# HGRN2 intra-chunk scores: 64 query columns per score matmul, shared PSUM banks, and a head's TensorE work in six bursts

## The chip, the cores and the metric

The kernel runs on one core of a Trainium2 chip. Its metric is the device time of one execution in microseconds (us). A core has five engines that run their own instruction queues in order: TensorE (PE, with its weight loads shown as PEld), VectorE (DVE), ScalarE (ACT), GpSimd (POOL) and SyncE (SP). Matmul results land in PSUM; the kernel keeps eight tiles of [128, 512] float32 there, one bank each, four for the projections (pool `pj`) and four for everything else (pool `pm`).

## What is computed

Two residual layers on a [512, 2048] float32 input: a recurrent layer (Griffin RG-LRU beside HGRN2, one input and one output projection), then differential attention. The part that matters is HGRN2, with 16 heads of 128 features, in chunks of 64 tokens:

```python
b = jnp.cumsum(gc, axis=2)                                   # log decay inside a chunk
o_inter = jnp.einsum('bhtk,bhkv->bhtv', qc * jnp.exp(b), state)
decay = jnp.exp(jnp.where(mask, b[:, :, :, None, :] - b[:, :, None, :, :], -jnp.inf))
scores = jnp.einsum('bhtk,bhsk,bhtsk->bhts', qc, kc, decay)
o = o_inter + jnp.einsum('bhts,bhsv->bhtv', scores, vc)
state = (jnp.exp(b_last[:, :, 0, :, None]) * state
         + jnp.einsum('bhsk,bhsv->bhkv', kc * jnp.exp(b_last - b), vc))
```

## The kernel before

Every projection is done in float32 by three float32r products of split operands: `split` (L91, L92) makes the weight tiles `whi` on ACT and `wlo` on DVE, five buffers each, and `mm3` (L104 to L106) multiplies. A raw weight chunk gives two half chunks of 12 matmuls with 512 columns each; these are the `pj` matmuls of the trace. All input projections of the HGRN2 heads come first (pairs of heads, 24 half chunks for q, f and gate, and 16 more for v in every second pair), then those of RG-LRU, then the output projection, then attention.

A head's own work is a Python generator, `hgrn_head`. After each half chunk, `tick(2)` runs two steps of the oldest unfinished head (a step ends at a `yield`). Before, a head has 24 steps, so two heads fill 24 half chunks. The Tile scheduler then orders each engine's queue, with the weight splits at high priority; it may move a step's instructions past some projection matmuls.

Inside a chunk the decay is not separable, so scores are built by levels of half block size h = 32, 16, 8, 4, 2, each from one tile `e` [128 features, 512 tokens]: in every block of 2h tokens the first h columns hold decayed keys and the last h decayed queries. `decays(h)` makes it: two subtractions or additions on DVE (L238, L239), an Exp on ACT (L240), a product with q on DVE (L241). `scores` multiplies `e` with itself, for h < 32 in four 128 x 128 products (L258); a float32 matmul is two instructions on PE, so one level is 8 LDWEIGHTS and 8 MATMUL. `copy_predicated` (L265) then takes the query columns of the level's blocks into the score tile `st`. The level h = 32 uses eight 32 x 32 products (L251). The products for s = t and s = t - 1 are sums over the features by a matrix of ones (L271 to L277).

After the levels come the 64 x 64 products between the two chunks of a 128-token pair (L318), transposes of the decayed keys `kp` (L325), the state products (L332, each followed by a DVE update, L334 and L336), the output product of scores and state (L343, L345) and its norm. The norm is: four squares with a sum on ACT (L350), a reciprocal square root by Newton steps on DVE (L115 to L122, twelve small instructions in a chain), the product `kp <- pm, rs_y` on DVE (L354), four transposes on PE (L359), and the product with gain and gate (L363). On ACT the functions Exp, Ln and Silu lie in different tables; a change of table is an ACT_TABLE_LOAD instruction in ACT's queue. The log decay of the next head takes Abs, Exp, Ln on ACT (L206 to L208) and then L209 on DVE.

Of the kernel before, what the change touches and what calls it, by code (L numbers as in the profile page):

```python
# [19 lines left out]
P = 128  # L20
# [15 lines left out]
# steps of the heads' own work between two half chunks of a projection  # L36
# [10 lines left out]
# columns of the packed constants  # L47
# [4 lines left out]
class Kernel:  # L52
# [73 lines left out]
    def proj_feat(self, h, src, chunk0, ticks):  # L126
        """256 output features as two [feature, token] banks"""
# [13 lines left out]
    def proj_tok(self, lhs, order, src, chunk0, ticks):  # L141
        """512 output features as four [token, feature] banks; lhs(kt) gives the split activations"""
# [14 lines left out]
    def prepare(self):  # L157
        """1 / rms of each token, as columns and as a row repeated for every partition; small constants"""
# [37 lines left out]
    def hgrn_head(self, hd, qs, f, sg, v, vc):  # L196
        nc, wk, sm, pm = self.nc, self.wk, self.sm, self.pm
        V = nc.vector
        # the lower bound is a softmax over one layer less its first row: it is zero
        # for these shapes, so log_f = log_sigmoid(f) and k = sigmoid(-f)  # L200
# [10 lines left out]
        # the scale of q goes with k  # L211
# [5 lines left out]
        # s = t, and s = t - 1 for odd t: products summed over the features by ones  # L217
# [26 lines left out]
        def scores(li, h, e):  # L244
            ps = pm.tile([P, S], F32, name="pm")
            if h == 32:
                ev, pv = (y.rearrange("p (a c) -> p a c", a=NT) for y in (st, ps))
# [5 lines left out]
                for o in (0, 64):  # L253
                    V.tensor_copy(ev[o:o + 32, :, o + 32:o + 64], pv[o:o + 32, :, o + 32:o + 64])
# [6 lines left out]
            def v4(t):  # L261
                return t.rearrange("p (a n two h) -> p a n two h", a=NT, two=2, h=h)[:, :, :, 1, :]
# [18 lines left out]
        yield
        for li, h in enumerate(LEVELS[1:], 1):
            pend.append((li, h, decays(h)))
            yield
            scores(*pend.pop(0))
            yield
        # pairs of 64-token chunks: k decayed to the end of its even chunk, q from the start of
        # its odd one; then both for the 128-token chunks, which meet through a running state
# [33 lines left out]
        so = wk.tile([P, 768], F32, name="so")
        ps = pm.tile([P, S], F32, name="pm")
        for c in range(NT - 1):
            nc.tensor.transpose(ps[:, c * P:(c + 1) * P], kp[:, c * P:(c + 1) * P], self.ident)  # L325
        nc.scalar.copy(so[:, 0:384], ps[:, 0:384])
# [75 lines left out]
    def rg_lambda(self):  # L402
        """-8 * softplus(-lambda), with log1p as 2 atanh(e / (2 + e))"""
# [24 lines left out]
    def rg_head(self, hd, xr, sg):  # L428
# [110 lines left out]
    def att_pair(self, pr, q, k, v, box):  # L539
# [7 lines left out]
        def heads_in(hh):  # L547
            """split transposes of a head's q and k"""
# [148 lines left out]
    def run(self):  # L697
# [20 lines left out]
        with ExitStack() as st:  # L718
# [3 lines left out]
            # products that nothing reads warm the array up while the first loads are under way  # L722
# [43 lines left out]
            # x1 = x + y @ w_out, its split transpose times the gain, and its mean squares  # L766
# [83 lines left out]
def feat_chunks(w, c0):  # L850
    """[2048, 256] at column c0 -> 4 chunks of four k tiles"""
# [3 lines left out]
def tok_chunks(w, c0, order=None):  # L855
    """[k, 512] at column c0 -> chunks of two k tiles, in the order of use"""
# [7 lines left out]
def layout(x, rec_norm, rec_w_in, rg_conv_w, rg_conv_b, rg_w_gate_a, rg_b_gate_a, rg_w_gate_x, rg_b_gate_x,  # L864
# [14 lines left out]
    gate = np.stack([rg_w_gate_a[0], rg_w_gate_x[0]], 1)                     # head, gate, i, j  # L879
# [41 lines left out]
```

## Time and profile before

| what | value |
|---|---|
| time, median of 3 runs (lowest to highest) | 2596.68 us (2595.3 to 2596.8) |
| span of the profiled execution | 2594.6 us |
| PE busy | 2579.6 us (99%), 12416 MATMUL |
| PEld busy | 2126.2 us (82%), 12416 LDWEIGHTS |
| DVE busy, ACT busy | 1417.0 us (55%), 1258.6 us (49%) |
| granted TensorE clock, mean | 0.998 of 2.4 GHz |
| L258 MATMUL, the score levels | 512, 67.5 us busy |
| L240 Exp of the levels on ACT | 80, 50.5 us busy |

The span of the profiled execution is 2.1 us under the median. A MATMUL's duration includes a part that overlaps with the next one, so what an instruction costs is read from the distance between starts, not from its duration. Starts are given to 0.01 us in the timelines.

### The profile page before, as it was taken

What the parts mean: (1) busy time and instruction counts of PE and PEld (TensorE: products, weight loads), DVE (VectorE), ACT (ScalarE), POOL (GpSimd) and SP (SyncE); (2) the same over time, 40 slices, a digit from 0 to 9 for tenths busy, and PEclk for the clock granted to TensorE, in tenths of its full rate; (3) what the DMA queues carried; (4) which work ended last, traced back from release to release, by engine and by line L of the source; (5) the groups of instructions that cost most, each with busy time, mean ns of one, the idle gap of its engine ahead of it and who ended that gap; (6) DMA issues with size and microseconds to landing.
All of it is one profiled execution on the core that took longest, in us unless ns stands there. A gap on an engine that the chain in (4) does not pass through costs nothing.

```text
span 2594.6 us, 33221 instructions
## 1 busy us (share of the span) xinstructions
PE 2579.6 (99%) x12416; PEld 2126.2 (82%) x12416; DVE 1417.0 (55%) x3073; ACT 1258.6 (49%) x2458; POOL 4.6 (0%) x12
## 2 busy tenths in 40 slices
PE   9999999999999999999999999999999999999999
PEld 7888888888888888888888888888888888888887
DVE  5466557646646665545654555344544534544654
ACT  8445545535444455556544444334434434534543
POOL 0000000000000000000000000000000000000000
PEclk9999999999999999999999999999999999999999
DMA  6222222222222222222232333222222222222243
GB/s 244 96 74 82 81 82 74 81 90 74 76 95 74 74 98 102 97 93 98 90 128 95 127 130 120 98 98 75 81 97 77 79 91 82 76 95 93 86 146 114
DMA packets 73457, 250.48 MB, mean 97 GB/s; under 512 B 8144, under 2 KB 8656, under 8 KB 73296
## 3 DMA queue, kind: packets, MB, share of 16 engines
q1 hardware_dynamic: 71712, 243.58, 26.8%
q0 software_dynamic: 1152, 4.19, 0.4%
q8 instruction: 97, 1.59, 0.2%
q10 hardware_dynamic: 432, 0.59, 0.1%
q14 instruction: 64, 0.52, 0.1%
HBM read 239.95 MB, written 8.39 MB: 96 GB/s over the span
## 4 chain that ended last, share of the span: by engine, by line
PE 94%; DVE 2%; ACT 2%; DMA 1%; issue 1%; SPq 0%; ACTq 0%
PE pj L104 28%; PE pj L106 28%; PE pj L105 28%; PE pm L258 2%; PE pm L570 1%; PE pm L104 1%; PE pm L106 1%; PE pm L105 1%; PE pm L343 1%; PE pm L554 1%; DMA yb<-in_x 0%; PE pm L332 0%; PE pm L345 0%; ACT a L675 0%; PE pm L359 0%
## 5 line engine op out<-in xcount | busy, mean ns | idle before, releaser
L92 DVE TENSOR_TENSOR wlo<-wraw,whi 128x512 fp32r<-128x512 f32 x848 | 582.3, 688 | 671.4 <-ACT whi L91 641.2
L91 ACT CAST whi<-wraw 128x512 fp32r<-128x512 f32 x848 | 523.0, 618 | 765.0 <-PE pj L106 463.7
L106 PE MATMUL pj<-whi,wlo 128*128 128x512 f32 x768 | 299.6, 390 | 0.0
L105 PE MATMUL pj<-wlo,whi 128*128 128x512 f32 x768 | 299.4, 390 | 0.0
L104 PE MATMUL pj<-whi 128*128 128x512 f32 x768 | 299.3, 390 | 0.0
L106 PEld LDWEIGHTS pj<-whi,wlo 128*128 128x128 f32 x768 | 144.2, 188 | 30.5 <-DVE wlo L92 0.6
L104 PEld LDWEIGHTS pj<-whi 128*128 128x128 f32 x768 | 144.2, 188 | 30.4 <-issue 0.5
L105 PEld LDWEIGHTS pj<-wlo,whi 128*128 128x128 f32 x768 | 144.2, 188 | 29.1
L240 ACT ACTIVATE e<-e 128x512 f32<-128x512 f32 x80 | 50.5, 632 | 131.7 <-DVE e L239 97.6
L92 DVE TENSOR_TENSOR wlo<-ya,whi 128x512 fp32r<-128x512 f32 x64 | 44.3, 693 | 89.9 <-ACT whi L91 89.9
L92 DVE TENSOR_TENSOR wlo<-y,whi 128x512 fp32r<-128x512 f32 x64 | 44.2, 691 | 82.3 <-ACT whi L91 82.3
L91 ACT CAST whi<-ya 128x512 fp32r<-128x512 f32 x64 | 39.7, 621 | 100.9 <-PE pj L105 100.9
L91 ACT CAST whi<-y 128x512 fp32r<-128x512 f32 x64 | 39.9, 623 | 94.1 <-PE pj L105 90.2
L92 DVE TENSOR_TENSOR wlo<-yb,whi 128x512 fp32r<-128x512 f32 x64 | 44.1, 690 | 72.2 <-ACT whi L91 72.0
L91 ACT CAST whi<-yb 128x512 fp32r<-128x512 f32 x64 | 39.8, 621 | 76.5 <-PE pj L105 76.5
L258 PEld LDWEIGHTS pm<-e 128*128 128x128 f32 x512 | 66.6, 191 | 5.0 <-DVE e L241 0.3
L258 PE MATMUL pm<-e 128*128 128x128 f32 x512 | 67.5, 275 | 0.0
L241 DVE TENSOR_TENSOR e<-e,hin 128x256 f32<-128x256 f32 x80 | 33.6, 420 | 58.8 <-ACT e L240 58.8
L575 ACT ACTIVATE p<-pm,mx 128x128 f32<-128x128 f32 (+3 forms) x64 | 33.7, 526 | 40.6 <-DVE mx L573 38.6
L572 DVE TENSOR_REDUCE mx<-pm 128x1 f32<-128x128 f32 (+3 forms) x64 | 30.4, 485 | 32.6 <-PE pm L571 32.3
L675 ACT ACTIVATE a<-pj,rstd 128x128 f32<-128x128 f32 x128 | 47.3, 421 | 0.3
L104 PE MATMUL pj<-h0h,whi 128*128 128x512 f32 x80 | 33.8, 423 | 5.2 <-DVE hin L384 2.9
(474 smaller groups left out, 6483.0 us busy)
## 6 DMA issues: line engine op xcount, KB each, us to landing
wraw<-in_w_rec SPq DMA_DIRECT2D x192, 512.0 KB, 3.2
wraw<-in_w_att SPq DMA_DIRECT2D x128, 512.0 KB, 3.2
wraw<-in_w_rout SPq DMA_DIRECT2D x64, 512.0 KB, 3.2
wraw<-in_w_aout SPq DMA_DIRECT2D x32, 512.0 KB, 3.2
yb<-in_xT SPq DMA_DIRECT2D x8, 512.0 KB, 8.5
yb<-in_x POOLq DMA_DIRECT2D x8, 512.0 KB, 5.5
wraw<-in_w_gate SPq DMA_DIRECT2D x8, 512.0 KB, 3.2
xo<-in_x SPq DMA_DIRECT2D x16, 256.0 KB, 4.0
```

Of the source, the lines that this page charges most:

```text
L91: self.nc.scalar.copy(hi, src)
L92: self.nc.vector.tensor_tensor(lo, src, hi.bitcast(F32), op=ALU.subtract)
L104: mm(out, a[0], b[0], start=start, stop=False)
L105: mm(out, a[0], b[1], start=False, stop=False)
L106: mm(out, a[1], b[0], start=False, stop=stop)
L240: nc.scalar.activation(e, e, AF.Exp)
L241: V.tensor_tensor(e1, e1, vw(qs, h)[:, :, 1, :], op=ALU.mult)
L258: nc.tensor.matmul(ps[:, sl], e[:, sl], e[:, sl], start=True, stop=True)
L343: nc.tensor.matmul(po[:, sl], st[:, sl], v[:, t, vc:vc + P], start=True, stop=t == 0)
L572: V.tensor_reduce(mx[:, i:i + 1], ps[:, :n], axis=AX.X, op=ALU.max)
L575: nc.scalar.activation(e[:, :n], ps[:, :n], AF.Exp, scale=ATT_SCALE, bias=mx[:, i:i + 1], accum_out=z[:, i:i + 1])
L675: nc.scalar.activation(x[:, t, g * P:(g + 1) * P], ps[t][:, g * P:(g + 1) * P], AF.Square, scale=r1, accum_out=ss[:, t * 4 + g:t * 4 + g + 1])
```

## The change

The tile `e` and its making stay as they are. `scores` becomes two functions. `score_mm` multiplies all 128 columns of a block of `e` as weights with only its 64 query columns (a strided view) as the moving operand, and writes 64 columns. Two levels of 256 columns share one bank. The level h = 32 writes 32 columns for each token tile beside the s = t - 1 sums in the same bank. `score_out` copies from the packed columns. The steps are regrouped: the sums and h = 32 in one step, h = 16 and 8 in one, and h = 4, h = 2, the 64 x 64 products and the transposes of `kp` in one, with three banks. A head has 22 steps instead of 24. Comments are removed; nothing else is touched.

```diff
-        def scores(li, h, e):
-            ps = pm.tile([P, S], F32, name="pm")
+        def score_mm(h, e, ps):
             if h == 32:
...
-                        nc.tensor.matmul(ps[o:o + 32, c + 32:c + 64], e[:, c:c + 32], e[:, c + 32:c + 64],
+                        nc.tensor.matmul(ps[o:o + 32, t * 32:(t + 1) * 32], e[:, c:c + 32], e[:, c + 32:c + 64],
                                          start=True, stop=True)
...
-                nc.tensor.matmul(ps[:, sl], e[:, sl], e[:, sl], start=True, stop=True)
+                nc.tensor.matmul(ps[:, t * 64:(t + 1) * 64], e[:, sl], vw(e[:, sl], h)[:, :, 1, :],
+                                 start=True, stop=True)
+
+        def score_out(li, h, ps):
...
+            dst = st.rearrange("p (a n two h) -> p a n two h", a=NT, two=2, h=h)[:, :, :, 1, :]
             mk = self.msk[:, li * 64:(li + 1) * 64].rearrange("p (n h) -> p n h", h=h)
-            V.copy_predicated(v4(st), mk.unsqueeze(1).broadcast_to([P, NT, n4, h]), v4(ps))
+            V.copy_predicated(dst, mk.unsqueeze(1).broadcast_to([P, NT, n4, h]),
+                              ps.rearrange("p (a n h) -> p a n h", a=NT, h=h))
...
+        e32 = decays(32)
+        yield
+        e16 = decays(16)
         yield
...
+        score_mm(32, e32, p2[:, 256:384])
...
+        score_out(0, 32, p2[:, 256:384])
+        yield
+        e8 = decays(8)
+        yield
+        e4 = decays(4)
+        yield
...
+        score_mm(16, e16, ps[:, 0:256])
+        score_mm(8, e8, ps[:, 256:512])
+        score_out(1, 16, ps[:, 0:256])
+        score_out(2, 8, ps[:, 256:512])
+        yield
+        e2 = decays(2)
+        yield
...
+        score_mm(4, e4, ps[:, 0:256])
+        score_mm(2, e2, ps[:, 256:512])
         for t in range(NT):
-            nc.tensor.matmul(ps[0:64, t * P + 64:(t + 1) * P], ke[:, t, :], qo[:, t, :], start=True, stop=True)
+            nc.tensor.matmul(p2[0:64, t * 64:(t + 1) * 64], ke[:, t, :], qo[:, t, :], start=True, stop=True)
+        for c in range(NT - 1):
+            nc.tensor.transpose(p3[:, c * P:(c + 1) * P], kp[:, c * P:(c + 1) * P], self.ident)
...
+        nc.scalar.copy(so[:, 0:384], p3[:, 0:384])
+        yield
         yield
```

In the changed file the lines shift: L258 becomes L255 (`score_mm`), L318 is L337, L325 is L339, L332 is L352, L343 and L345 are L363 and L365, L350 is L370, L354 is L374, L359 is L379 and L384 is L404. L91, L92, L104 to L106, L115 to L122 and L206 to L209 keep their numbers.

How it moves the rows, for the sixth head (the second of its pair). First PE's queue before, around the last score level and the 64 x 64 products (L258 scores, L318 and L325 as above, the rest projection):

```order
L106 MATMUL pj<-h7h,wlo 128x512
L258 MATMUL pm<-e 128x128 x4
L104 MATMUL pj<-h8h,whi 128x512
L105 MATMUL pj<-h8l,whi 128x512
L106 MATMUL pj<-h8h,wlo 128x512
```

and, twelve projection matmuls further on:

```order
L105 MATMUL pj<-h9l,whi 128x512
L106 MATMUL pj<-h9h,wlo 128x512
L318 MATMUL pm<-e_3370 64x64 x4
L325 MATMUL pm<-cst,kp 128x128 x3
L104 MATMUL pj<-h10h,whi 128x512
L105 MATMUL pj<-h10l,whi 128x512
```

PE's queue now, at the same place of the same head:

```order
L105 MATMUL pj<-h5l,whi 128x512
L106 MATMUL pj<-h5h,wlo 128x512
L255 MATMUL pm<-e 128x64 x8
L337 MATMUL pm<-e_3273 64x64 x4
L339 MATMUL pm<-cst,kp 128x128 x3
L104 MATMUL pj<-h6h,whi 128x512
```

Two levels, the 64 x 64 products and the transposes now stand in one piece, where three pieces stood with twelve projection matmuls between each two.

DVE's queue before, from the first sums of the norm's chain to its end (L354), in the same head:

```order
L122 SCALAR_TENSOR_TENSOR rs_y<-rs_t,rs_y 128x4
L384 TENSOR_TENSOR hin_3530<-pj,rrow 128x512
L120 TENSOR_TENSOR rs_t<-rs_y 128x4
L227 TENSOR_TENSOR e_3592<-so,e_3586 128x768
L92 TENSOR_TENSOR wlo<-wraw,whi 128x512
L121 TENSOR_TENSOR rs_t<-rs_t,rs_m 128x4
L313 TENSOR_TENSOR qp<-qp,hin_3027 128x4x64
L122 SCALAR_TENSOR_TENSOR rs_y<-rs_t,rs_y 128x4
L120 TENSOR_TENSOR rs_t<-rs_y 128x4
L121 TENSOR_TENSOR rs_t<-rs_t,rs_m 128x4
L122 SCALAR_TENSOR_TENSOR rs_y<-rs_t,rs_y 128x4
L92 TENSOR_TENSOR wlo<-wraw,whi 128x512
```

DVE's queue now, at the same place, up to L374:

```order
L122 SCALAR_TENSOR_TENSOR rs_y<-rs_t,rs_y 128x4
L227 TENSOR_TENSOR e_3574<-so,e_3568 128x768
L92 TENSOR_TENSOR wlo<-wraw,whi 128x512
L120 TENSOR_TENSOR rs_t<-rs_y 128x4
L121 TENSOR_TENSOR rs_t<-rs_t,rs_m 128x4
L209 SCALAR_TENSOR_TENSOR lf<-hin_3293,lf 128x512
L122 SCALAR_TENSOR_TENSOR rs_y<-rs_t,rs_y 128x4
L374 TENSOR_TENSOR kp<-pm,rs_y 128x512
```

Now L209 of the next head stands inside the chain, between its last L121 and L122; before, it came after L354. On ACT the instructions that L209 waits for stand like this now, behind the squares of the same norm:

```order
L222 ACTIVATE so<-lf 128x256
L311 ACTIVATE qp<-b 128x512
L206 ACTIVATE lf<-hin_3293 128x512
L225 CAST e_3568<-so 128x768
L91 CAST whi<-wraw 128x512
L207 ACTIVATE lf<-lf 128x512
L208 ACT_TABLE_LOAD
L208 ACTIVATE lf<-lf 128x512
```

Before, L207 and L208 of the next head came three splits later, after L354's place. PE's transposes L379 stand 29 projection matmuls behind the head's output product in the second head of a pair (L359 stood 34 behind) and 23 in the first (27 before). In the whole program ACT has 132 ACT_TABLE_LOAD rows, where it had 118; from RG-LRU's later heads on, the queues are the same as before.

## Rows read from the trace of the kernel before

**Rows 1.** Windows view, the steady part of the HGRN2 stage: length, then busy us of PE, PEld, DVE, ACT, POOL with the number of instructions, granted clock, DMA share, GB/s.

```profile
175.00:915.00 740.00, 738.52 (x3957) 611.89 (x3956) 461.79 (x1068) 365.08 (x680) 0.00 (x0) 1.00 0.23 79
```

**Rows 2.** The chain of work that ended last, shares of the span by engine (from the page).

```profile
PE 94%; DVE 2%; ACT 2%; DMA 1%; issue 1%; SPq 0%; ACTq 0%
```

**Rows 3.** Groups by line, shapes kept apart, from 130 to 915 us: the score levels and the 64 x 64 products. Columns: line, engine, operation, names, weights' size, shape, count, busy us, mean ns of one, idle before.

```profile
L258 PE MATMUL pm<-e 128*128 128x128 f32 x512 | 67.5, 275 | 0.0
L258 PEld LDWEIGHTS pm<-e 128*128 128x128 f32 x512 | 66.6, 191 | 5.0 <-DVE e L241 0.3
...
L318 PE MATMUL pm<-e 128*64 128x64 f32 x128 | 10.9, 228 | 0.0
L318 PEld LDWEIGHTS pm<-e 128*64 128x64 f32 x128 | 8.6, 137 | 5.4 <-PE pj L105 5.3
```

**Rows 4.** Timeline of PE in the HGRN2 stage: start us, length us, engine, line, operation, names, shape, count. A row with x8 or x16 runs from the first start to the last end.

```profile
401.02 1.05 PE L258 MATMUL pm<-e 128*128 128x128 f32 x8
401.83 0.48 PE L104 MATMUL pj<-h6h,whi 128*128 128x512 f32 x1
402.14 0.39 PE L105 MATMUL pj<-h6l,whi 128*128 128x512 f32 x1
...
404.44 0.39 PE L106 MATMUL pj<-h7h,wlo 128*128 128x512 f32 x1
...
408.40 0.68 PE L318 MATMUL pm<-e 128*64 128x64 f32 x8
...
419.93 0.39 PE L104 MATMUL pj<-h0h,whi 128*128 128x512 f32 x1
...
422.42 0.39 PE L106 MATMUL pj<-h1h,wlo 128*128 128x512 f32 x1
...
429.45 0.40 PE L104 MATMUL pj<-h6h,whi 128*128 128x512 f32 x1
...
432.01 0.39 PE L106 MATMUL pj<-h7h,wlo 128*128 128x512 f32 x1
432.32 0.45 PE L251 MATMUL pm<-e 128*32 128x32 f32 x16
432.70 0.50 PE L104 MATMUL pj<-h8h,whi 128*128 128x512 f32 x1
433.04 0.39 PE L105 MATMUL pj<-h8l,whi 128*128 128x512 f32 x1
```

**Rows 5.** Timeline of PE in the attention stage, where L571 adds the causal mask with a bfloat16 matmul of 128 columns and a projection matmul with 128 float32r weight columns follows.

```profile
1759.27 0.23 PE L571 MATMUL pm<-neg_b,ident_b 128*128 128x128 bf16 x1
...
1759.62 0.39 PE L105 MATMUL pj<-wlo,h5h 128*128 128x512 f32 x1
```

**Rows 6.** Timeline of PE and DVE in the first head of a pair, from the output product (L343) to the transposes (L359), and of PE at the transposes of the last head of all. In brackets: idle before, and what ended it.

```profile
162.44 0.61 PE L343 MATMUL pm<-v,st 128*128 128x128 f32 x4
...
165.73 0.42 DVE L223 TENSOR_TENSOR so<-so,hin 128x256 f32<-128x256 f32 x1
...
169.26 0.16 DVE L121 TENSOR_TENSOR rs_t<-rs_t,rs_m 128x4 f32<-128x4 f32 x1
...
169.45 0.16 DVE L122 SCALAR_TENSOR_TENSOR rs_y<-rs_t,rs_y 128x4 f32<-128x4 f32 x1
...
169.65 0.69 DVE L354 TENSOR_TENSOR kp<-pm,rs_y 128x512 f32<-128x512 f32 x1
...
169.95 0.39 PE L106 MATMUL pj<-h10h,wlo 128*128 128x512 f32 x1
...
170.26 0.68 DVE L92 TENSOR_TENSOR wlo<-wraw,whi 128x512 fp32r<-128x512 f32 x1
...
170.49 0.63 PE L359 MATMUL pm<-cst,kp 128*128 128x128 f32 x4 [0.15 <-DVE kp L354]
...
913.82 0.39 PE L106 MATMUL pj<-h6h,wlo 128*128 128x512 f32 x1
914.49 0.63 PE L359 MATMUL pm<-cst,kp 128*128 128x128 f32 x4 [0.28 <-DVE kp L354]
```

**Rows 7.** Timeline of PE, ACT and DVE in the second head of a pair, from the output product on.

```profile
415.61 0.61 PE L343 MATMUL pm<-v,st 128*128 128x128 f32 x4
...
418.38 0.45 ACT L222 ACTIVATE so<-lf 128x256 f32<-128x256 f32 x1
...
420.55 0.62 ACT L91 CAST whi<-wraw 128x512 fp32r<-128x512 f32 x1
...
424.69 0.39 PE L104 MATMUL pj<-h3h,whi 128*128 128x512 f32 x1
...
425.09 0.63 PE L359 MATMUL pm<-cst,kp 128*128 128x128 f32 x4
425.47 0.63 ACT L207 ACTIVATE lf<-lf 128x512 f32<-128x512 f32 x1
...
426.00 0.61 ACT L91 CAST whi<-wraw 128x512 fp32r<-128x512 f32 x1
426.63 1.28 ACT L208 ACT_TABLE_LOAD   x1
427.92 0.63 ACT L208 ACTIVATE lf<-lf 128x512 f32<-128x512 f32 x1
...
428.58 0.69 DVE L209 SCALAR_TENSOR_TENSOR lf<-hin,lf 128x512 f32<-128x512 f32 x1 [0.88 <-ACT lf L208]
```

More of the change, by code (lines that the diff above doesn't have):

```diff
@@ L242, in decays @@
             return e
-        def scores(li, h, e):
-            ps = pm.tile([P, S], F32, name="pm")
+        def score_mm(h, e, ps):
             if h == 32:
-                ev, pv = (y.rearrange("p (a c) -> p a c", a=NT) for y in (st, ps))
                 for t in range(NT):
@@ L257, in scores @@
                 sl = slice(t * P, (t + 1) * P)
-                nc.tensor.matmul(ps[:, sl], e[:, sl], e[:, sl], start=True, stop=True)
+                nc.tensor.matmul(ps[:, t * 64:(t + 1) * 64], e[:, sl], vw(e[:, sl], h)[:, :, 1, :],
+                                 start=True, stop=True)
+        def score_out(li, h, ps):
+            if h == 32:
+                ev, pv = st.rearrange("p (a c) -> p a c", a=NT), ps.rearrange("p (a c) -> p a c", a=NT)
+                for o in (0, 64):
+                    V.tensor_copy(ev[o:o + 32, :, o + 32:o + 64], pv[o:o + 32])
+                return
             n4 = P // (2 * h)
-            def v4(t):
-                return t.rearrange("p (a n two h) -> p a n two h", a=NT, two=2, h=h)[:, :, :, 1, :]
+            dst = st.rearrange("p (a n two h) -> p a n two h", a=NT, two=2, h=h)[:, :, :, 1, :]
             mk = self.msk[:, li * 64:(li + 1) * 64].rearrange("p (n h) -> p n h", h=h)
-            V.copy_predicated(v4(st), mk.unsqueeze(1).broadcast_to([P, NT, n4, h]), v4(ps))
-        pend = [(0, LEVELS[0], decays(LEVELS[0]))]
+            V.copy_predicated(dst, mk.unsqueeze(1).broadcast_to([P, NT, n4, h]),
[3 more added lines that the diff above has]
+        e16 = decays(16)
         yield
@@ L270, in hgrn_head @@
         ps = pm.tile([P, S], F32, name="pm")
+        p2 = pm.tile([P, S], F32, name="pm")
         nc.tensor.matmul(ps, self.ones, xh[:, 0:512], start=True, stop=False)
         nc.tensor.matmul(ps, self.ones, xl[:, 0:512], start=False, stop=True)
+        nc.tensor.matmul(p2[:, 0:256], self.ones, xh[:, 512:768], start=True, stop=False)
+        nc.tensor.matmul(p2[:, 0:256], self.ones, xl[:, 512:768], start=False, stop=True)
+        score_mm(32, e32, p2[:, 256:384])
         V.tensor_tensor(st.rearrange("p (a c) -> p a c", a=NT), ps.rearrange("p (a c) -> p a c", a=NT),
                         self.ident.unsqueeze(1).broadcast_to([P, NT, P]), op=ALU.mult)
-        ps = pm.tile([P, S], F32, name="pm")
-        nc.tensor.matmul(ps[:, 0:256], self.ones, xh[:, 512:768], start=True, stop=False)
-        nc.tensor.matmul(ps[:, 0:256], self.ones, xl[:, 512:768], start=False, stop=True)
         V.copy_predicated(st.rearrange("p (a n two) -> p a n two", a=NT, two=2)[:, :, :, 1],
                           self.msk[:, 64 * len(LEVELS):].unsqueeze(1).broadcast_to([P, NT, 64]),
-                          ps[:, 0:256].rearrange("p (a n) -> p a n", a=NT))
+                          p2[:, 0:256].rearrange("p (a n) -> p a n", a=NT))
+        score_out(0, 32, p2[:, 256:384])
         yield
[L282 to L286, printed above, removed]
+        e8 = decays(8)
+        yield
+        e4 = decays(4)
+        yield
         kp = wk.tile([P, S], F32, name="kp")
@@ L305, in hgrn_head @@
         nc.scalar.activation(qp, b, AF.Exp)
+        yield
+        ps = pm.tile([P, S], F32, name="pm")
+        score_mm(16, e16, ps[:, 0:256])
[5 more added lines that the diff above has]
+        yield
         nc.scalar.activation(ke, c64(kp)[:, :, 0, :], AF.Exp)
         nc.scalar.activation(c64(kp)[:, :, 1, :], c64(kp)[:, :, 1, :], AF.Exp)
+        V.tensor_tensor(qo, c64(qp)[:, :, 1, :], c64(qs)[:, :, 1, :], op=ALU.mult)
         yield
-        scores(*pend.pop(0))
-        yield
-        V.tensor_tensor(qo, c64(qp)[:, :, 1, :], c64(qs)[:, :, 1, :], op=ALU.mult)
         V.tensor_tensor(c64(kp)[:, :, 0, :], ke, dc[:, 1:8:2].unsqueeze(2).broadcast_to([P, 4, 64]), op=ALU.mult)
@@ L315, in hgrn_head @@
         yield
+        yield
         ps = pm.tile([P, S], F32, name="pm")
+        p2 = pm.tile([P, S], F32, name="pm")
+        p3 = pm.tile([P, S], F32, name="pm")
+        score_mm(4, e4, ps[:, 0:256])
+        score_mm(2, e2, ps[:, 256:512])
         for t in range(NT):
-            nc.tensor.matmul(ps[0:64, t * P + 64:(t + 1) * P], ke[:, t, :], qo[:, t, :], start=True, stop=True)
+            nc.tensor.matmul(p2[0:64, t * 64:(t + 1) * 64], ke[:, t, :], qo[:, t, :], start=True, stop=True)
+        for c in range(NT - 1):
+            nc.tensor.transpose(p3[:, c * P:(c + 1) * P], kp[:, c * P:(c + 1) * P], self.ident)
+        score_out(3, 4, ps[:, 0:256])
+        score_out(4, 2, ps[:, 256:512])
         nc.scalar.copy(st.rearrange("p (a c) -> p a c", a=NT)[0:64, :, 64:128],
-                       ps.rearrange("p (a c) -> p a c", a=NT)[0:64, :, 64:128])
+                       p2[0:64, 0:256].rearrange("p (a c) -> p a c", a=NT))
+        so = wk.tile([P, 768], F32, name="so")
+        nc.scalar.copy(so[:, 0:384], p3[:, 0:384])
         yield
[L322 to L326, printed above, removed]
         yield
```

2 lines of the change are left out of this document (removed).

## The prediction

> **What bounds the kernel now.** I read first the windows of the HGRN2 stage, since the change touches nothing else. In 740 us of it PE is busy for 738.52 us at a granted clock of 1.00, DVE for 462 and ACT for 365 [rows 1], and the chain that ended last is 94% PE [rows 2]. So time is won here by a shorter PE queue, and lost where PE has to wait. Next I read the groups of the score levels [rows 3], then PE's timeline around the pieces that the change merges [rows 4], one place in the attention stage that shows what a short moving operand is worth [rows 5], and last the two places where PE waits in every head: the transposes L359 [rows 6, 7].
>
> **The score matmuls stream half the columns: no gain.** A level costs 8 pairs of LDWEIGHTS and MATMUL. Eight MATMULs take 401.83 - 401.02 = 0.81 us to the next projection matmul; inside, starts are (1.05 - 0.275) / 7 = 0.111 us apart [rows 3, 4]. The L318 products, with half the weight columns and half the moving columns, are (0.68 - 0.228) / 7 = 0.065 us apart, an upper end since the first is longer [rows 3, 4]. The question is which of the two halves buys this. The change halves only the moving columns; the weights are still all 128 columns of a block. A LDWEIGHTS of 128 columns lasts 191 ns and one of 64 columns 137 ns, 54 ns less, 0.84 ns per column, so 128 columns take 0.84 x 128 = 108 ns of the load path, which is the distance of the starts [rows 3]. That a load isn't hidden by a short stream is seen twice. After the 32 x 32 products PE has run empty; the first L104 then starts at 432.70 and the next at 433.04, 0.34 us instead of the 0.227 of a quiet stretch: 0.11 us in which PE waits for 128 weight columns [rows 4]. And L571 streams 128 bfloat16 columns, with a MATMUL of 0.23 us as short as that of L318 (0.228), before a load of 128 columns: L571 and L104 together take 1759.62 - 1759.27 = 0.35 us, no less than the last score matmul with L104 (402.14 - 401.80 = 0.34, with its start at 401.02 + 7 x 0.111) [rows 3 to 5]. A slot of the score burst is the longer of this stream and the next load, and the load stays. So 512 instructions at 0.111 us before are 512 at 0.111 us after: 0. The bounds are 0 and 512 x (0.111 - 0.065) = 24 us of gain; I take 0, because rows 5 have the same load behind a short stream.
>
> [...]
>
> Strided moving operands are nowhere in the trace. Reading all 128 columns instead of 64 would cost what a slot costs before, 0.111 us, so this too lies between 0 and the slot that the load sets. The packed PSUM columns move DVE's copies (L265) by some tenths of a us per head at most; they lie beside PE's projection matmuls, twelve or more of which follow each burst before anything reads `st`.
>
> **Merging the bursts: 3.2 us less.** Twelve projection matmuls take 422.42 - 419.93 = 2.49 us from first to last start in a quiet stretch, 404.44 - 401.83 = 2.61 after a score burst and 432.01 - 429.45 = 2.56 after the sums [rows 4]. Of the 0.12 behind a score burst some 0.08 is the last slot (0.111 less the 0.03 already spent), which stays; 0.035 is lost per burst. Sums and h = 32 in one: 0.06 less. Levels 16 and 8 in one: 0.03 less. Levels 4 and 2 and the 64 x 64 products in one: two of 0.035, and the run-empty ahead of the narrow tiles (432.32 - 432.01 = 0.31 instead of 0.227 [rows 4]) is some 0.05 shorter behind a 64-column stream: 0.11. Together 0.20 us per head, 16 heads: 3.2 us. Bounds: 0, if the loss goes with the slots and not with the bursts, and 16 x 0.24 = 3.9, if the run-empty ahead of the narrow tiles (0.08) goes whole.
>
> **PE's wait for the norm: 8 us more.** PE waits at L359 in every head: the transposes start 0.15 us after the end of L354 (169.65 + 0.69 = 170.34, then 170.49), while the matmul before would let them start at 169.95 + 0.227 = 170.18: 0.31 us in the first head of a pair [rows 6]; and 425.09 - (424.69 + 0.227) = 0.17 in the second [rows 7]. Now in the second heads the transposes come 29 projection matmuls behind the output product instead of 34: PE is there 5 x 0.227 earlier, 9.31 - 1.13 = 8.17 us after the first L363, where 9.31 is 424.92 - 415.61. DVE's chain is the list that the first head has before, in the same order (L121 at 169.26, 6.82 us after L343, L354 ending at 7.90 [rows 6]), so by itself it would make it. But L209 now stands between L121 and L122 and waits for ACT, and there a table load lies in front of the Ln. ACT's order is that of rows 7 up to the split at 420.55, 4.94 us after L343. From there, by rows 7: split to L207 0.51 (an instruction is followed 0.1 before its end, as L207 at 425.47 by the split at 426.00), L207 to the table load 0.64 (its length; a load waits for it), load to L208 1.29, L208 0.63: L208 ends at 8.02. L209 starts 0.03 later (428.58 against 428.55), holds DVE for 0.61 (as L354 does, 169.65 to 170.26), L122 to L374 takes 0.20 (169.45 to 169.65), L374 0.69 [rows 6]: end at 9.55, transposes at 9.70. Wait: 9.70 - 8.17 = 1.53 us instead of 0.17. Seven second heads (all but the last) have this order: 7 x 1.36 = 9.5 us more. A wait of PE is paid in full there: nothing else is in its queue ahead of the transposes.
>
> In the first heads PE comes 23 matmuls after the product instead of 27, at 7.74 - 0.91 = 6.83 us. A table load now stands ahead of L222 (2.77 + 1.29 = 4.07 to 4.2, where 2.77 is 418.38 - 415.61; end 0.45 later, at 4.65 [rows 7]); then L223 and L224 (at most 0.42 each), L122, a split (0.61) and L374 (0.69) [rows 6]: end at 6.8 to 6.95, wait 0.1 to 0.25 instead of 0.31, seven times: 0.8 us less. The last two heads have neither a load nor L209 in the chain; the 15th loses a wait like that of a first head, 0.31, and the last one of 914.49 - 913.82 - 0.227 = 0.44 [rows 6]: 0.7 less. Together + 9.5 - 0.8 - 0.7 = + 8.0 us.
>
> **What hides the rest.** 14 table loads more (132 against 118) are 14 x 1.29 = 18 us of ACT, which is busy for half of the stage [rows 1]; outside the two chains above they lie under the splits, which run five half chunks ahead of PE. Bursts come every two or three half chunks instead of every one, with e made at least one before: no new wait there, and if e4 or e2 came late, it would be late by tenths of a us. States, output products and DVE's updates keep their distance of one half chunk (2.7 us).
>
> Sum: 2594.6 (span) - 3.2 + 8.0 = 2599.4; the median lies 2.1 us over the span, so **2601.5 us**, 0.18% above 2596.68. About 0.2%, 5.2 us, is what a measurement of this kernel can tell from no change: the forecast lies just inside it.
>
> **Rivals.**
> 1. Slower: the merge gives nothing back. The loss of 0.035 to 0.06 us after a burst then belongs to its matmuls and the refill behind them, and is as long after 16 as after 8. For it: after the 16 instructions of L251 it is no longer than after 8. Against: it is read once per burst, whatever its length. Time 2601.5 + 3.2 = 2604.7, 0.3% slower; it decides once the merge gives less than 2.7 us.
> 2. Faster: the load isn't what paces a score slot, and 64 columns shorten it to that of L318, 24 us less: 2577.5. For it: L318 itself, and that load and stream are equally long in rows 3, so that they can't be told apart there. Against: rows 5 and the wait at 432.70.
> 3. The wait for the norm stays as it was in the second heads, because L208 is early enough or L209 isn't in the way: 9.5 less, 2592.0, 0.18% faster. Against: L208 to L209 is back to back in rows 7, and the order is fixed in the queues.
> 4. More heads wait, in the first ones too, by a table load (1.29 us x 7 = 9 us): 2610.5. Only if ACT came to L222 late.
>
> **How the numbers follow.** Forecast 0.56, its own range 2599 to 2604: 0.36 of it within 0.2% and 0.20 above, since the bound lies 0.4 us over the forecast and its unknowns are mostly waits. Rival 1: 0.20, slower. Rival 2: 0.10, faster. Rival 3: 0.10, of it 0.06 within. Rival 4: 0.04, slower. So slower by over 0.2%: 0.20 + 0.20 + 0.04 = 0.44; within: 0.36 + 0.06 = 0.42; faster: 0.10 + 0.04 = 0.14. The range of 8 in 10 leaves out rivals 2 and 4 and takes in 1 and 3: 2590 to 2607.
>
> **What would show it.** Starts of L255 0.111 us apart, with MATMULs of some 228 ns and LDWEIGHTS at 191; PE idle ahead of L379 of about 1.5 us in seven heads, released by L374, with L209 ahead of it on DVE; 0.1 to 0.25 in the others; 2.61 us for twelve matmuls after each merged burst. Starts near 0.06 apart would make the prediction wrong by 24 us; L209 ending before 6.8 us would take away the 9.5.

## The result and the profile after

The changed kernel takes **2602.64 us** (median of 13 runs, 2600.64 to 2603.41) against 2596.28 for the kernel before (13 runs beside it, 2595.28 to 2596.97): a ratio of 1.0022, 95% interval 1.0015 to 1.0029. It is slower by 6.4 us, by the median just above the bound of 0.2% (5.2 us), with the interval on both sides of it, and 1.1 us over the forecast. The profiled execution took 2603.31 us with a span of 2601.5, against 2594.6 before. Of these 6.9 us, 1.1 is there before the heads' own work has begun (the same projection matmul starts at 57.88 instead of 56.78 us), in a stretch that the change doesn't touch and that moves by over 2 us between the profiles of this case; 5.7 come in the HGRN2 stage, and nothing behind it.

PE has 93% of the chain that ended last, 94% before [rows 2]. The window of [rows 1] in the kernel after:

```profile
175.00:915.00 740.00, 729.64 (x3919) 611.34 (x3914) 462.30 (x1054) 383.09 (x682) 0.00 (x0) 1.00 0.23 79
```

PE's busy time there was 738.52 [rows 1] and is 729.64 us, with the clock at 1.00: PE stands still for nearly 9 us more. The view of PE's waits, from 130 to 915 us, names the line (what waited <- whom it waited for: us in total, times, longest):

```profile
PE pm L379 <- DVE kp L374: 9.7, 8, 1.4
```

L379 is the transposes, L359 before. The score levels by line, shapes kept apart, as in [rows 3]:

```profile
L255 PE MATMUL pm<-e 128*128 128x64 f32 x512 | 60.6, 271 | 0.0
L255 PEld LDWEIGHTS pm<-e 128*128 128x128 f32 x512 | 62.1, 191 | 2.4
```

and the timeline of PE at a merged burst, as in [rows 4]:

```profile
403.61 1.89 PE L255 MATMUL pm<-e 128*128 128x64 f32 x16
...
406.35 0.48 PE L104 MATMUL pj<-h6h,whi 128*128 128x512 f32 x1
...
408.95 0.39 PE L106 MATMUL pj<-h7h,wlo 128*128 128x512 f32 x1
```

The MATMULs now stream 64 columns, yet the mean is 271 ns and 16 of them last 1.89 us from the first start to the last end: (1.89 - 0.27) / 15 = 0.108 us apart in the mean, with 0.27 the length of the last. One distance, the first, is short (0.055 us); the other fourteen are 0.110 to 0.116. That is the slot (the distance between two starts) of [rows 3, 4]. The loads still last 191 ns. Twelve projection matmuls behind the burst take 408.95 - 406.35 = 2.60 us, as before behind a burst half as long.

Timeline of PE, ACT and DVE in the second head of a pair, from the output product (L363, L343 before) on, as in [rows 7]:

```profile
412.62 0.61 PE L363 MATMUL pm<-v,st 128*128 128x128 f32 x4
...
418.08 0.63 ACT L207 ACTIVATE lf<-lf 128x512 f32<-128x512 f32 x1
...
418.73 1.28 ACT L208 ACT_TABLE_LOAD   x1
...
419.44 0.16 DVE L121 TENSOR_TENSOR rs_t<-rs_t,rs_m 128x4 f32<-128x4 f32 x1
...
420.02 0.63 ACT L208 ACTIVATE lf<-lf 128x512 f32<-128x512 f32 x1
...
420.58 0.39 PE L105 MATMUL pj<-h14l,whi 128*128 128x512 f32 x1
420.69 0.69 DVE L209 SCALAR_TENSOR_TENSOR lf<-hin,lf 128x512 f32<-128x512 f32 x1 [1.09 <-ACT lf L208]
421.30 0.15 DVE L122 SCALAR_TENSOR_TENSOR rs_y<-rs_t,rs_y 128x4 f32<-128x4 f32 x1
421.49 0.69 DVE L374 TENSOR_TENSOR kp<-pm,rs_y 128x512 f32<-128x512 f32 x1
...
422.32 0.63 PE L379 MATMUL pm<-cst,kp 128*128 128x128 f32 x4 [1.36 <-DVE kp L374]
```

DVE has L121 done at 419.60 and then stands still for 1.09 us, because the next instruction in its queue is L209 of the next head, and the Ln that feeds L209 sits behind a table load on ACT. L374 ends at 422.18, 9.56 us after the first L363; PE, which could have begun at 420.58 + 0.227 = 420.81, begins at 422.32: 1.51 us lost here, 1.51 to 1.53 in all seven heads of this kind. In the first head of a pair:

```profile
160.61 0.61 PE L363 MATMUL pm<-v,st 128*128 128x128 f32 x4
...
163.53 1.28 ACT L222 ACT_TABLE_LOAD   x1
...
166.89 0.68 DVE L374 TENSOR_TENSOR kp<-pm,rs_y 128x512 f32<-128x512 f32 x1
...
167.21 0.39 PE L105 MATMUL pj<-h7l,whi 128*128 128x512 f32 x1
...
167.71 0.63 PE L379 MATMUL pm<-cst,kp 128*128 128x128 f32 x4
```

167.71 - 167.21 - 0.227 = 0.27 us, where it was 0.31 [rows 6]. Read this way (start of the transposes less the start of the matmul before less 0.228), the 16 waits add up to 13.5 us, against 4.2 before: 9.3 more. The stage got 5.7 longer; so some 3.5 came back, from the merged bursts (run 7).

### The profile page after: what moved, and what is told of

Same layout as the page of the kernel before. It is cut to its first block, busy times and chain, and to the rows that moved or that the text cites. A ratio compares the mean times of both kernels' runs of the same rounds, so it can differ in the third digit from the quotient of the medians.

```text
span 2601.5 us, 33160 instructions
## 1 busy us (share of the span) xinstructions
PE 2575.9 (99%) x12416; PEld 2128.9 (82%) x12416; DVE 1420.9 (55%) x3073; ACT 1282.2 (49%) x2472; POOL 4.6 (0%) x12
## 4 chain that ended last, share of the span: by engine, by line
PE 93%; ACT 3%; DVE 2%; issue 1%; DMA 0%; SPq 0%; ACTq 0%
PE pj L104 28%; PE pj L106 28%; PE pj L105 27%; PE pm L255 2%; PE pm L590 1%; PE pm L104 1%; PE pm L106 1%; PE pm L105 1%; ACT a L695 1%; PE pm L363 1%; ACT whi L91 0%; PE pm L574 0%; PE pm L365 0%; PE pm L352 0%; PE pm L379 0%
## 5 line engine op out<-in xcount | busy, mean ns | idle before, releaser
L92 DVE TENSOR_TENSOR wlo<-wraw,whi 128x512 fp32r<-128x512 f32 x848 | 582.4, 688 | 717.3 <-ACT whi L91 677.6
L91 ACT CAST whi<-wraw 128x512 fp32r<-128x512 f32 x848 | 523.5, 618 | 789.3 <-PE pj L106 479.8
L106 PE MATMUL pj<-whi,wlo 128*128 128x512 f32 x768 | 299.6, 390 | 0.0
L104 PE MATMUL pj<-whi 128*128 128x512 f32 x768 | 299.4, 390 | 0.0
L104 PEld LDWEIGHTS pj<-whi 128*128 128x128 f32 x768 | 144.2, 188 | 30.5 <-issue 0.5
L106 PEld LDWEIGHTS pj<-whi,wlo 128*128 128x128 f32 x768 | 144.1, 188 | 30.5 <-DVE wlo L92 0.6
L92 DVE TENSOR_TENSOR wlo<-ya,whi 128x512 fp32r<-128x512 f32 x64 | 44.3, 692 | 89.9 <-ACT whi L91 89.9
L91 ACT CAST whi<-ya 128x512 fp32r<-128x512 f32 x64 | 39.7, 621 | 100.9 <-PE pj L105 100.9
L92 DVE TENSOR_TENSOR wlo<-y,whi 128x512 fp32r<-128x512 f32 x64 | 44.2, 691 | 82.4 <-ACT whi L91 82.3
L91 ACT CAST whi<-y 128x512 fp32r<-128x512 f32 x64 | 39.9, 623 | 94.1 <-PE pj L105 90.2
L92 DVE TENSOR_TENSOR wlo<-yb,whi 128x512 fp32r<-128x512 f32 x64 | 44.1, 690 | 72.3 <-ACT whi L91 72.1
L91 ACT CAST whi<-yb 128x512 fp32r<-128x512 f32 x64 | 39.8, 621 | 76.5 <-PE pj L105 76.5
L255 PEld LDWEIGHTS pm<-e 128*128 128x128 f32 x512 | 62.1, 191 | 2.4
L255 PE MATMUL pm<-e 128*128 128x64 f32 x512 | 60.6, 271 | 0.0
L267 DVE COPY_PREDICATED st<-msk,pm 128x256 f32<-128x256 int32 x64 | 32.4, 506 | 12.8 <-PE pm L255 12.8
```

What stands on the lines that cost most here:

```text
L91: self.nc.scalar.copy(hi, src)
L92: self.nc.vector.tensor_tensor(lo, src, hi.bitcast(F32), op=ALU.subtract)
L104: mm(out, a[0], b[0], start=start, stop=False)
L106: mm(out, a[1], b[0], start=False, stop=stop)
L255: nc.tensor.matmul(ps[:, t * 64:(t + 1) * 64], e[:, sl], vw(e[:, sl], h)[:, :, 1, :], start=True, stop=True)
L267: V.copy_predicated(dst, mk.unsqueeze(1).broadcast_to([P, NT, n4, h]), ps.rearrange("p (a n h) -> p a n h", a=NT, h=h))
```

## The experiments

The theory: a score slot is the longer of its stream and the next weight load, so halving the stream alone gives nothing; each merge saves the loss behind one burst (an unbroken row of such small matmuls between projection matmuls); the rest is PE's wait for a norm that L209 holds up. The rivals of the prediction stand against each part. All eight runs are told, each against the kernel before on the same chip, 2596.3 to 2596.5 us.

### 1. The halved stream alone

```diff
-                nc.tensor.matmul(ps[:, sl], e[:, sl], e[:, sl], start=True, stop=True)
+                nc.tensor.matmul(ps[:, t * 64:(t + 1) * 64], e[:, sl], vw(e[:, sl], h)[:, :, 1, :],
+                                 start=True, stop=True)
...
```

The cut lines make the masked copy read the packed columns.

> The kernel before with one edit: the score matmuls of levels 16 to 2 take as moving operand the 64 query columns of a block instead of all 128, with the same 128 weight columns, and the masked copy reads the packed 256 columns. Order, bursts and table loads are those of before. Theory (a slot is the longer of its stream and the next weight load, and the load is the longer): starts inside the burst stay 0.112 us apart, MATMULs of some 228 instead of 275 ns, LDWEIGHTS 191; eight of them reach to the next projection matmul in 0.90 us as before; the time is that of before, 2596.3 (within 0.05%). Rival (the stream paces): starts near 0.06 apart, 512 x 0.046 to 0.053 = 24 to 27 us less, 2569 to 2572.

Measured: 2596.22 us, ratio 0.9999 (0.9990 to 1.0008). The groups:

```profile
L258 PE MATMUL pm<-e 128*128 128x64 f32 x512 | 64.0, 268 | 0.0
L258 PEld LDWEIGHTS pm<-e 128*128 128x128 f32 x512 | 66.7, 191 | 4.8
```

The median distance of starts inside a burst is 0.112 us, before it was 0.111, and eight of them reach to the next projection matmul in 0.81 us in both (not the 0.90 of the expectation, see [rows 4]). Rival 2 is out, and strided moving operands cost nothing that shows. One expectation missed: the MATMULs don't shorten to 228 ns, they stay at 268 in the mean; with the same 64 columns they last 227 in run 3, behind narrow weights, so their recorded length isn't set by the stream alone.

### 2 and 3. Narrow weights, with the full and with the halved stream

```diff
-                nc.tensor.matmul(ps[:, sl], e[:, sl], e[:, sl], start=True, stop=True)
+                nc.tensor.matmul(ps[0:64, sl], e[:, t * P:t * P + 64], e[:, sl], start=True, stop=True)
...
```

Rows 64 to 127 of these scores are neither computed nor copied, in this run and the next.

> The kernel before, but the score matmuls of levels 16 to 2 take only the first 64 columns of a block as weights and all 128 as moving columns; the rows 64 to 127 of their scores are left out of the result. Theory (the longer of the two): the stream is now the longer one. A MATMUL of 128 columns lasts 275 ns and one of 64 lasts 228, 0.73 ns a column, so the slot is 0.094 to 0.111 us: 0 to 9 us less, 2587 to 2596. Rival A (the load alone paces, a stream is free): slot 0.058 to 0.065, 24 to 27 us less, about 2571. Rival B (the stream alone paces): 0.111, 2596.

Run 3 takes both 64 weight columns and the 64 moving columns of run 1.

> The kernel before, but the score matmuls of levels 16 to 2 take 64 weight columns and 64 moving columns; the rows 64 to 127 of their scores are left out of the result. All theories but one: slot 0.056 to 0.065 as in the 64 x 64 products, 512 x (0.111 - 0.060) = 24 to 28 us less, 2568 to 2572. It is the difference of this run from the two others that tells: if it alone gains, a slot is the longer of load and stream; if the run with narrow weights gains as much, the load alone; if the run with the halved stream does, the stream alone. The one that falls with no gain here: a fixed price of 0.11 us for an instruction, whatever its size.

Measured: 2615.80 us for narrow weights alone, 1.0075 (1.0063 to 1.0088), and 2588.58 for both, 0.9969 (0.9956 to 0.9981). Groups, narrow weights first, then both:

```profile
L258 PE MATMUL pm<-e 128*64 128x128 f32 x480 | 65.2, 279 | 0.0
L258 PEld LDWEIGHTS pm<-e 128*64 128x64 f32 x480 | 50.8, 136 | 21.1 <-issue 10.9 <-DVE e L239 3.9 <-DVE wlo L92 2.5
```

```profile
L258 PE MATMUL pm<-e 128*64 128x64 f32 x512 | 43.2, 227 | 0.0
L258 PEld LDWEIGHTS pm<-e 128*64 128x64 f32 x512 | 34.5, 137 | 21.9 <-issue 9.9 <-DVE e L239 4.9 <-DVE st L266 2.8
```

The median distance of starts inside a burst is 0.109 us with 64 weight and 128 moving columns, and 0.058 with 64 and 64. With the 0.112 of run 1 (128 weight, 64 moving) that is all four corners: either full side alone keeps the slot at 0.11, only both halved shorten it. The theory of the slot stands.

The times missed, both on the slow side, for a reason that no theory had. A burst of narrow weights starts late and leaves late. Timeline of PE with narrow weights alone, then with both halves:

```profile
404.02 1.09 PE L258 MATMUL pm<-e 128*64 128x128 f32 x8
405.04 0.50 PE L104 MATMUL pj<-h4h,whi 128*128 128x512 f32 x1
```

```profile
402.18 0.39 PE L106 MATMUL pj<-h7h,wlo 128*128 128x512 f32 x1
402.50 0.68 PE L258 MATMUL pm<-e 128*64 128x64 f32 x8
403.11 0.50 PE L104 MATMUL pj<-h8h,whi 128*128 128x512 f32 x1
```

With both halves it is 402.50 - 402.18 = 0.32 us instead of 0.227 ahead of the burst, so 0.09 lost at the entry, and 0.61 from the first start to L104, where 8 slots of 0.058 would be 0.46. Against the 0.81 of before [rows 4] a burst gains 0.20 - 0.09 = 0.11 us; 64 such bursts, 7 us: the 7.7 measured. With the full stream a burst takes 405.04 - 404.02 = 1.02 us from its first start to L104 (the median of the 60 bursts before 915 us, too), 0.21 more than the 0.81 of before, plus the 0.09 of entry: 0.30 us more, times 64 is 19 us, the 19.5 measured. What makes the entry and the last slot of narrow weights long was not tested. So the 64 x 64 products in [rows 3], from which the prediction took its bound of 24 us, carry such an entry each time (0.32 us in the trace of the kernel before); the bound was the slot alone.

### 4. The logarithm of the next head starts behind the transposes

```diff
-        lf = wk.tile([P, S], F32, name="lf")
+        lf = wk.tile([P, S], F32, name="lf" if hd % 2 else "kp")
```

> The changed kernel with one edit: the first head of a pair takes its tile lf in the buffer of kp, which the norm of the head before it holds until its transposes, so that L206 to L209 of the next head start behind them and L209 no longer stands in the norm's chain on DVE. The table loads stay 132, and the bursts, slots and first heads are those of the changed kernel. The transposes then come 18 projection matmuls behind the output product. Theory (the added time is PE's wait for a norm that L209 holds up): DVE's chain ends some 3.5 us earlier, PE waits 0.2 to 0.4 us ahead of the transposes of seven heads instead of 1.52; 7 x 1.1 to 1.3 = 8 to 9 us less than the changed kernel, 2593.5 to 2594.8, 0.06 to 0.11% under the kernel before. Rival A (the added time is that of the 14 more table loads, or of the merged bursts): 2602.6 as before the edit. Rival B (the wait moves: the next head's first products come late, since its logarithm starts later): the wait ahead of L379 goes, and one as long stands ahead of L277; 2599 to 2603.

Measured: 2611.53 us, 1.0055 (1.0042 to 1.0067): slower than the changed kernel by 9 us. Ahead of L379 the theory held: the seven waits fell from 1.52 to 0.33 or 0.34 us (8.3 us less over all heads). But rival B came in, at a higher price than it gave. PE at the sums of the next head:

```profile
433.26 0.39 PE L106 MATMUL pj<-h5h,wlo 128*128 128x512 f32 x1
434.17 0.50 PE L277 MATMUL pm<-e,ones 128*128 128x512 f32 x1 [0.52 <-ACT e L225]
435.79 0.50 PE L278 MATMUL pm<-e,ones 128*128 128x512 f32 x1 [1.12 <-DVE e L227]
...
438.47 0.63 PE L104 MATMUL pj<-h6h,whi 128*128 128x512 f32 x1
438.89 0.63 PE L105 MATMUL pj<-h6l,whi 128*128 128x512 f32 x1
```

and the windows there (the granted clock is the third number from the end):

```profile
434.00:436.00 2.00, 0.71 (x2) 0.40 (x3) 2.00 (x5) 2.00 (x5) 0.00 (x0) 1.00 0.11 43
437.00:438.00 1.00, 1.00 (x6) 0.83 (x3) 1.00 (x3) 0.00 (x0) 0.00 (x0) 0.50 0.06 16
```

ACT and DVE are busy without a break while PE waits 0.68 us for the cast L225 and, behind it, 1.39 for the remainder L227, with 0.10 lost by the matmul after it (start less the start before less 0.228, the distance that these sums have in the changed kernel): 2.2 us at four places, 8.7 in all. Then matmuls come 0.43 us apart instead of 0.227 for some 3 us: PE had stood mostly idle from 433.5 to 436, and the clock fell from 1.00 to 0.50, the lower of the two levels (1.2 GHz). That happened at three of the four places and cost 1.5 to 1.6 us each, by the starts of the same matmuls in the changed kernel; at the first (220.77 us) the same waits left the clock at 1.00. With 0.58 us at three matmuls that wait for L404, these add up to 8.7 + 4.6 + 1.7 - 8.3 = 6.7 of the 7.1 us by which the work from 88.3 us on got longer. The two spans differ by 8.9, since the edit reached the first pair as well:

```profile
84.55 0.57 PE L104 MATMUL pj<-whi,h0h 128*128 128x512 f32 x1 [1.88 <-DVE hin L404]
```

There ACT's queue now has the second head's logarithm ahead of work of the first head (L213), and PE waits 1.88 us where it waited 0.26; the clock is at 0.50 from 85 to 88 us, and the place costs 3.2 us more than in the changed kernel, while the start-up ahead of it is 1.5 us shorter. So L209 is the cause of the wait at L379, and starting the logarithm late is no cure.

### 5. The transposes later

```diff
         yield
+        if hd % 2:
+            for _ in range(3):
+                yield
         ps = pm.tile([P, S], F32, name="pm")
         for t in range(NT):
             nc.tensor.transpose(ps[:, t * P:(t + 1) * P], on[:, t * P:(t + 1) * P], self.ident)
```

> The changed kernel with one edit: in the second head of a pair three empty steps stand ahead of the transposes, so that 36 projection matmuls instead of 29 lie between the output product and them. L209 stays inside the norm's chain on DVE, behind the Ln and its table load; the next head's logarithm isn't moved. Theory (the added time is that the transposes come too early for a chain that L209 holds up): L374 still ends 9.55 us after the first L363, PE comes there at 8.17 + 7 x 0.227 = 9.76 and waits for nothing; 7 x 1.52 = 10.6 us less than the changed kernel, 2592.0, 0.17% under the kernel before. Rival A (the time is in the bursts or in the table loads): 2602.6. Rival B (what follows the transposes comes late now, as the sums did when the logarithm was moved): the wait returns ahead of L277 of the next head, 2597 to 2611.

Measured: 2590.47 us, 0.9975 (0.9965 to 0.9986). The second head:

```profile
407.44 0.61 PE L363 MATMUL pm<-v,st 128*128 128x128 f32 x4
...
415.50 0.69 DVE L209 SCALAR_TENSOR_TENSOR lf<-hin,lf 128x512 f32<-128x512 f32 x1 [1.09 <-ACT lf L208]
...
416.30 0.69 DVE L374 TENSOR_TENSOR kp<-pm,rs_y 128x512 f32<-128x512 f32 x1
...
416.98 0.39 PE L106 MATMUL pj<-h15h,wlo 128*128 128x512 f32 x1
417.21 0.60 PE L382 MATMUL pm<-cst,kp 128*128 128x128 f32 x4
```

DVE's stall of 1.09 us is still there and L374 still ends 416.99 - 407.44 = 9.55 us after the first L363, but PE comes at 417.21 and waits for nothing (0 to 0.004 us in all seven). It is 12.2 us less than the changed kernel, where 10.6 was expected; the spans of the two profiles differ by 13.1, of which 10.9 lie in the stage and 2.1 in the start-up, which the edit doesn't touch. Rivals A and B fall: the bursts are untouched and no wait shows ahead of L277. Seven of the 132 table loads went too, but their number isn't it: run 6, with 100, is no faster.

### 6. The table load taken away

```diff
-        nc.scalar.activation(lf, lf, AF.Ln, bias=1.0)
+        nc.scalar.activation(lf, lf, AF.Exp)
```

> The changed kernel, but L208 computes Exp instead of Ln, so that no other table is needed there: the log of the forget gate isn't the reference's. Order on DVE and PE as in the changed kernel: L209 inside the chain, transposes 29 matmuls behind the product; 100 table loads instead of 132. Theory: L208 ends 1.3 us sooner, L209 then waits for DVE's own row instead (L121 ends at 6.96 us after the first L363), L374 ends at some 8.5 and the transposes start at 8.65: PE waits 0.3 to 0.5 us in the second heads, and 0 to 0.1 in the first, where the load ahead of L222 goes too. 7 x 1.1 + 7 x 0.2 = 9 us less than the changed kernel, about 2593.5. Rival (the place of L209 alone makes the wait, the load is hidden): more than 1.2 us in the second heads as before, 2601 to 2603.

Measured: 2592.28 us, 0.9985 (0.9976 to 0.9994), 10.4 less than the changed kernel, where 9 was expected; 8.8 of it lie in the stage by the two profiles. Second head:

```profile
407.56 0.61 PE L363 MATMUL pm<-v,st 128*128 128x128 f32 x4
...
413.69 0.63 ACT L208 ACTIVATE lf<-lf 128x512 f32<-128x512 f32 x1
414.38 0.16 DVE L121 TENSOR_TENSOR rs_t<-rs_t,rs_m 128x4 f32<-128x4 f32 x1
414.46 0.68 DVE L209 SCALAR_TENSOR_TENSOR lf<-hin,lf 128x512 f32<-128x512 f32 x1
...
415.25 0.69 DVE L374 TENSOR_TENSOR kp<-pm,rs_y 128x512 f32<-128x512 f32 x1
416.09 0.63 PE L379 MATMUL pm<-cst,kp 128*128 128x128 f32 x4 [0.18 <-DVE kp L374]
```

L209 stands in the same place, but no longer waits; L374 ends 8.38 us after the first L363 and PE waits 0.33 to 0.35 us instead of 1.52. So about 1.2 of the 1.5 us is the table load, and the place of L209 is what lets it in. The first heads, expected to fall to 0.1 or less, stayed at 0.27 to 0.28: contrary to what was expected, the table load ahead of L222 is still there (at 160.83 us, 1.28 long).

### 7. Two merges undone

On top of run 5, the 32 x 32 products go back to one half chunk behind the sums, and level 8 to one behind level 16:

```diff
-        score_mm(32, e32, p2[:, 256:384])
...
-        score_out(0, 32, p2[:, 256:384])
         yield
         e8 = decays(8)
         yield
+        ps = pm.tile([P, S], F32, name="pm")
+        score_mm(32, e32, ps[:, 256:384])
+        score_out(0, 32, ps[:, 256:384])
...
-        score_mm(8, e8, ps[:, 256:512])
...
-        score_out(2, 8, ps[:, 256:512])
         yield
         e2 = decays(2)
         yield
+        ps = pm.tile([P, S], F32, name="pm")
+        score_mm(8, e8, ps[:, 0:256])
+        score_out(2, 8, ps[:, 0:256])
```

> The kernel with the later transposes, but two of the merges undone: the 32 x 32 products come one half chunk behind the sums, and level 8 one behind level 16, as in the kernel before. Eight bursts in a head instead of six, the same matmuls. Theory (0.06 us and 0.03 us are lost per burst, by the twelve projection matmuls that follow): 16 x 0.09 = 1.5 us more than the kernel with the later transposes alone, 2593.5 if that one is at 2592.0; PE's rows show 2.56 and 2.61 us for twelve matmuls behind every one of the four bursts. Rival (the merge gives nothing): the same time within 0.3 us, and 2.53 to 2.55 us for twelve matmuls behind the smaller bursts.

Measured: 2592.09 us, 1.6 more than run 5, where 1.5 was expected; the two intervals overlap, so the rows decide. From the sums to the 24th projection matmul behind them, PE of run 5, then of this run:

```profile
381.71 0.39 PE L277 MATMUL pm<-e,ones 128*128 128x512 f32 x1
...
388.21 0.39 PE L106 MATMUL pj<-h15h,wlo 128*128 128x512 f32 x1
```

```profile
381.79 0.39 PE L277 MATMUL pm<-e,ones 128*128 128x512 f32 x1
...
385.35 0.45 PE L250 MATMUL pm<-e 128*32 128x32 f32 x16
...
388.35 0.39 PE L106 MATMUL pj<-h15h,wlo 128*128 128x512 f32 x1
```

6.50 against 6.56 us for the same work: 0.06 a head. Over the stage the traces give 0.065 for this merge and 0.033 for levels 16 and 8 (the stage of this run is 1.7 us longer in all), and the bursts of the kernels before and after give 0.125 for the last one, which no run took back by itself. Rival 1 falls: the loss goes with the number of bursts.

### 8. The first heads' transposes later too

```diff
-        if hd % 2:
-            for _ in range(3):
-                yield
+        for _ in range(3 if hd % 2 else 1):
+            yield
```

> The kernel with the later transposes in the second heads, and one empty step ahead of the transposes of the first heads too: 24 matmuls instead of 23 behind the output product there; the next head's first products come one half chunk later. Theory: PE comes at 7.06 us where L374 ends at 6.95 and the transposes could start at 7.09; the wait of 0.27 us in seven first heads falls to 0.05, 1.6 us less than with the later transposes alone: 2590.4 if that one is at 2592.0. Rival (the later sums move the next head's logarithm chain against ACT's table loads): PE waits ahead of L277 or L255, no gain or some us of loss.

Measured: **2588.62 us**, 0.9970 (0.9958 to 0.9981), 1.9 us under run 5 where 1.6 was expected, though their intervals overlap. In the first heads PE now comes one matmul later:

```profile
164.61 0.68 DVE L374 TENSOR_TENSOR kp<-pm,rs_y 128x512 f32<-128x512 f32 x1
...
165.16 0.39 PE L106 MATMUL pj<-h7h,wlo 128*128 128x512 f32 x1
...
165.44 0.63 PE L381 MATMUL pm<-cst,kp 128*128 128x128 f32 x4
```

165.44 - 165.16 - 0.227 = 0.05 us in all seven. The 16 waits add up to 1.2 us, 0.8 of it in the last two heads. Its median is the lowest of all kernels that compute every score (run 3, at 2588.58, leaves half of them out), below before and after; the changed kernel's merges pay once PE comes after the norm instead of before it.

## Why the prediction was right, step by step

- **Streaming half the columns, 0 us: right.** Run 1 shows it alone, runs 2 and 3 the reason. The Trainium skill (TensorE: Matmul & The Clock Gate, Back-to-back issue gap) says that in a stream of weight loads and matmuls the spacing is set by both, and gives a gap from the moving columns alone only for the isolated matmul; the four distances of runs 1 to 3 agree. By the Trainium skill (TensorE: Matmul & The Clock Gate, LDWEIGHTS) a load takes columns / 1.2 ns, an estimate of 107 ns for 128, which is near the 112 of run 1.
- **Merging, -3.2 us: right, 3.6 by the rows.** 0.065 + 0.033 + 0.125 = 0.22 us a head instead of 0.20, 16 heads; the last merge gave the most. (The bound of 16 x 0.24 is 3.8, not 3.9.)
- **PE's wait in the second heads, +9.5 us: right.** 7 x (1.52 - 0.17) = 9.4. L374 was put at 9.55 and the transposes at 9.70 us; both are there. Runs 5 and 6 show the two halves of the mechanism: PE's early arrival and the table load. Rival 3 falls by this wait.
- **The other heads, -1.5 us: wrong by 1.4, the term that was mis-sized.** First heads: 0.27 instead of the 0.1 to 0.25 forecast, so 0.3 us back and not 0.8. L374 ends 6.96 us after the first L363, at the late end of the 6.8 to 6.95 forecast, and from there the prediction's own working gives 6.95 + 0.15 - 6.83 = 0.27: its 0.25 was a slip, and its 0.8 took the middle of the range. Rival 4 falls by the same wait. Last two: from "The last two heads have neither a load nor L209 in the chain" the prediction took it that their waits go (0.7 us less), but they wait 0.32 and 0.57 us, where it had 0.31 and 0.44 before; in the 15th, L374 ends 7.90 us after the first L363, as it did in the first heads before [rows 6], and PE's transposes stand 27 projection matmuls behind, as before, so nothing there could shorten the wait.
- **The sum**: 4.8 forecast for the stage, 5.7 measured: the other heads cost 1.4 more than forecast, and the merges gave back 0.4 more. The median is 1.1 over the forecast, inside the range, and crossed the 0.2% bound by 1 us, which the interval doesn't settle. That it lies so near has luck in it, since the start-up moves by more than that. Part of what moves it shows in the granted clock: from some 57 us on it is at 0.50 for some 7 us in the profiles of both kernels and of runs 1 and 2, and for some 3 us in those of runs 3 to 8; between the changed kernel and run 5 this is 1.0 of the 2.1 us. What decides it, and what moves the rest, stays open; nothing was run on it.

## What to carry to other kernels

When one engine's instructions are moved, the queue of every other engine is rebuilt around them: read what now stands inside each dependent chain, and what that waits for. The wait that a chain put on the bound engine was cured here on the bound engine's side, by letting it come later, while moving the intruder moved the wait and cost the clock too. Halving one operand of these small matmuls bought nothing while the other operand was as long; ask which of load and stream paces the slot.

## What was not expected

- Narrow weights have a price of their own: 64 instead of 128 weight columns between 128-column matmuls lose 0.09 us at the entry (0.32 instead of 0.227), and the last slot takes 0.15 (64 moving columns) to 0.20 us (128) instead of the 0.03 that the last of 128 x 128 shows, so that a burst of 8 with 128 moving columns became 0.30 us longer by loading less.
- Twelve matmuls behind a burst take 2.61 us instead of 2.49 after 8 score matmuls and after 16 alike.
- In run 4, PE's two waits ahead of the sums were followed by the clock's lower level at three places of four, with some 1.5 us lost to slower matmuls each, beside the 2.2 us of the waits themselves; so was a single wait of 1.88 us at 84.55 us.
